# Splitting streamed weights into two parts: whole slots of 1024 columns instead of two halves

## The chip, the cores and the metric

The kernel runs on one core of one Trainium2 chip. The time is device microseconds of that core from the start to the end of one launch, the median of several executions. Before the change it is 2640.28 us (three runs, 2636.97 to 2641.47).

## What is computed

The reference is two transformer-like blocks in float32 over one sequence of 256 tokens and 1024 features, each of two layers. Cut to what matters here:

```
def first_block(x, mem, ...):
    for l in range(2):
        x = layer_norm(a * x + 0.5 * swiglu(x, ffn1_w1[l], ffn1_w3[l], ffn1_w2[l]))
        x = layer_norm(a * x + token_mixing(x, w_in[l], ...))       # gMLP, conv, MLA, NSA branches
        x = layer_norm(a * x + cross_attention(x, mem, ...))
        x = layer_norm(a * x + 0.5 * swiglu(x, ffn2_w1[l], ffn2_w3[l], ffn2_w2[l]))

def second_block(x, p, ...):
    for layer in range(2):
        x = half_ffn(x, ...)
        x = x + mixer(rmsnorm(x))          # layer 0: GLA + RG-LRU, layer 1: HGRN
        x = half_ffn(x, ...)
        x = x + sigmoid(rmsnorm(x) @ ple_gate[layer]) * (p[layer] @ ple_proj[layer])
    return rmsnorm(x)
```

Nearly all the work is products of the 256 x 1024 activations with weight matrices that are read once each from HBM: feed-forward matrices of 1024 x 2816 (24 of them), the input projection of token mixing, and smaller ones.

## The kernel before, in words

**Three products for one.** Products run in the type float32r. To keep float32 accuracy each operand is split into a part `hi` (the value cast to float32r) and a rest `lo` (value minus `hi`), and `mm3` (L187) computes hi·hi + hi·lo + lo·hi: L190, L191 and L192 are its three matmuls. Activations are split when they are transposed (`split_to`, L258; `rms_prep`, L327); weights are split as they stream in.

**Slots.** A slot is 128 partitions x up to 1024 columns of weights, 512 KB. `slot` (L167) starts the DMA on the SP queue into a raw buffer `raw` (pool of 4), ScalarE casts it into `whi` (L176) and VectorE subtracts into `wlo` (L177); both of these pools hold 8. Before the change each slot of n columns is split in two halves of n/2: cast, subtraction, cast, subtraction. A full slot feeds 12 matmuls of 512 columns: two k-blocks (or two column halves), two token tiles, three products.

**Token tiles.** The 256 tokens are two tiles t = 0, 1 of 128 rows. `lin` (L194) and `ffn` (L360) loop over slots and use each for both tiles. `lin_rows` (L224) makes the last product of a stage: it keeps the last `skew` slots, finishes tile 0, calls `done(0)`, and runs tile 1's share of these slots while tile 0 is normalised; then comes `done(1)`, while TensorE begins the next stage with tile 0's 24 matmuls.

**The end of a stage.** In the first block `done` is `layer_norm` (L293). On tile 1 it is a chain over four engines: two sums on VectorE (L299, one per half), the mean in two tiny steps (L302, L303), the sum of squares on ScalarE (`lnj`, L306), its scaling on VectorE (`rs`, L308), a power on GpSimd (L309), and the normalisation on VectorE, L313 with the mean and L314 with `rs`; then TensorE transposes (L318 here, L335 in `rms_prep`) and the result is split into `xT` (L259 and L260, or L339 and L340). In the second block `done` adds the residual, transposes, splits with a gain (`rms_prep`) and takes the sum of squares on ScalarE (`junk`, L325).

**Order.** The program is recorded in the order of the code and put in its final order, engine by engine, by a scheduler with its own estimates of durations; `issue_after` pins a few places. Each engine then works its list in order, so a weight cast or subtraction stands at a fixed place among the steps of a normalisation and everything behind it waits with it. Side work (attention, recurrences) is woven between slots by `weave` (L85).

Of the kernel before, what the change touches and what calls it, by code (L numbers as in the profile page):

```python
# [94 lines left out]
class Core:  # L95
    def __init__(self, tc, ctx, a):
        self.tc, self.a = tc, a
        nc = self.nc = tc.nc
        self.V, self.A, self.G, self.T = nc.vector, nc.scalar, nc.gpsimd, nc.tensor
        e = ctx.enter_context  # L100

        self.wsp = e(tc.tile_pool(name="wsp", bufs=8))
        self.xp = e(tc.tile_pool(name="xp", bufs=1))
        self.bp = e(tc.tile_pool(name="bp", bufs=11))
        self.cst = e(tc.tile_pool(name="cst", bufs=1))
        self.wraw = e(tc.tile_pool(name="wraw", bufs=4))
        self.rp = e(tc.tile_pool(name="rp", bufs=2))
        self.gbp = e(tc.tile_pool(name="gbp", bufs=1))
        self.sc2 = e(tc.tile_pool(name="sc2", bufs=6))
        self.sc4 = e(tc.tile_pool(name="sc4", bufs=2))  # L110
        self.biasp = e(tc.tile_pool(name="biasp", bufs=2))
        self.smp = e(tc.tile_pool(name="smp", bufs=5))
        self.accp = e(tc.tile_pool(name="accp", bufs=4, space=PSUM))
        self.atp = e(tc.tile_pool(name="atp", bufs=2, space=PSUM))
        self.tpp = e(tc.tile_pool(name="tpp", bufs=2, space=PSUM))
        self.ident = self.const("c_ident")
        self.mhalf = self.cst.tile([P, 32], F32, name="mhalf")
        self.V.memset(self.mhalf, -0.5)
        self.one = self.cst.tile([P, 1], F32, name="one")
        self.V.memset(self.one, 1.0)  # L120
# [46 lines left out]
    def slot(self, parts, n):  # L167

        raw = self.wraw.tile([P, 1024], F32, tag="raw", name="raw")
        hi = self.wsp.tile([P, 1024], F32R, tag="whi", name="whi")  # L170
        lo = self.wsp.tile([P, 1024], F32R, tag="wlo", name="wlo")
        for view, src in parts(raw):
            self.nc.sync.dma_start(out=view, in_=src)
        m = n // 2
        for v in (slice(0, m), slice(m, n)):
            self.A.copy(hi[:, v], raw[:, v])  # L176
            self.V.tensor_sub(lo[:, v], raw[:, v], hi[:, v].bitcast(F32))  # L177
        return hi, lo
# [1355 lines left out]
```

## Time and profile before

| | |
|---|---|
| median of three runs | 2640.28 us |
| the profiled execution | 2640.52 us |
| its span in the trace | 2638.7 us |
| TensorE busy in the span | 2597.5 us, 98% |
| VectorE busy | 1648.4 us, 62% |
| ScalarE busy | 1398.0 us, 53% |
| granted TensorE clock, mean | 0.997 |
| weight casts (L176) and subtractions (L177) | 1682 each |

The trace is of one execution. A group of instructions is named by its line in the code, its engine and the tiles it writes and reads; a duration of one instruction includes some latency that overlaps the next one, so a pair of two takes less than twice one. An engine's idle time is put down to what ended it. TensorE's matmuls overlap each other and their ends are modelled, so "busy" there says that the engine had work, not that it ran at its peak.

### The profile page before, as it was taken

What the parts mean: (1) busy time and instruction counts of PE and PEld (TensorE: products, weight loads), DVE (VectorE), ACT (ScalarE), POOL (GpSimd) and SP (SyncE); (2) the same over time, 40 slices, a digit from 0 to 9 for tenths busy, and PEclk for the clock granted to TensorE, in tenths of its full rate; (3) what the DMA queues carried; (4) which work ended last, traced back from release to release, by engine and by line L of the source; (5) the groups of instructions that cost most, each with busy time, mean ns of one, the idle gap of its engine ahead of it and who ended that gap; (6) DMA issues with size and microseconds to landing.
All of it is one profiled execution on the core that took longest, in us unless ns stands there. A gap on an engine that the chain in (4) does not pass through costs nothing.

```text
span 2638.7 us, 35816 instructions
## 1 busy us (share of the span) xinstructions
PE 2597.5 (98%) x12833; PEld 2141.8 (81%) x12833; DVE 1648.4 (62%) x3232; ACT 1398.0 (53%) x2795; POOL 76.2 (3%) x122
## 2 busy tenths in 40 slices
PE   8999999999999999999999999999999999999998
PEld 7888877887888889877878878887888788777887
DVE  6557676766556557677675565567655655565554
ACT  5445545555445445545565455456554655765544
POOL 0000000000000000001000000000000000001000
PEclk9999999999999999999999999999999999999999
DMA  8648564546657557554456556554655665455652
GB/s 282 186 157 225 169 187 128 155 152 196 188 168 215 184 168 218 163 169 132 135 182 195 191 174 193 195 168 130 181 185 172 199 184 197 146 166 146 188 191 96
DMA packets 261800, 465.42 MB, mean 176 GB/s; under 512 B 25963, under 2 KB 96118, under 8 KB 261622
## 3 DMA queue, kind: packets, MB, share of 16 engines
q1 hardware_dynamic: 261622, 463.13, 57.7%
q8 instruction: 101, 1.65, 0.3%
q14 instruction: 77, 0.63, 0.1%
HBM read 462.02 MB, written 1.05 MB: 175 GB/s over the span
## 4 chain that ended last, share of the span: by engine, by line
PE 88%; DVE 5%; ACT 3%; DMA 2%; issue 1%; POOL 1%; POOLq 0%; DVEq 0%; ACTq 0%; SPq 0%
PE h L190 11%; PE h L192 11%; PE h L191 11%; PE o L190 7%; PE o L191 7%; PE o L192 7%; PE lin L190 6%; PE lin L192 6%; PE lin L191 6%; PE tp L268 2%; PE linT L220 1%; PE linT L219 1%; PE linT L218 1%; PE sp L447 1%; DVE wlo L177 1%
## 5 line engine op out<-in xcount | busy, mean ns | idle before, releaser
L177 DVE TENSOR_TENSOR wlo<-raw,whi 128x512 fp32r<-128x512 f32 (+3 forms) x1682 | 1100.1, 688 | 723.2 <-ACT whi L176 719.7
L176 ACT CAST whi<-raw 128x512 fp32r<-128x512 f32 (+3 forms) x1682 | 963.6, 616 | 892.3 <-PE h L192 366.4
L190 PE MATMUL h<-whi,xT 128*128 128x512 f32 x1280 | 504.0, 394 | 2.4 <-ACT whi L176 1.2
L192 PE MATMUL h<-whi,xT 128*128 128x512 f32 x1280 | 499.5, 391 | 0.8 <-DVE xT L260 0.8
L191 PE MATMUL h<-wlo,xT 128*128 128x512 f32 x1280 | 499.1, 390 | 0.0
L190 PEld LDWEIGHTS h<-whi,xT 128*128 128x128 f32 x1280 | 240.8, 188 | 55.8 <-ACT xT L339 4.9
L192 PEld LDWEIGHTS h<-whi,xT 128*128 128x128 f32 x1280 | 240.6, 188 | 52.7 <-DVE xT L260 1.7
L191 PEld LDWEIGHTS h<-wlo,xT 128*128 128x128 f32 x1280 | 241.0, 188 | 48.6
L190 PE MATMUL o<-whi,gT 128*128 128x512 f32 x704 | 275.7, 392 | 0.0
L191 PE MATMUL o<-wlo,gT 128*128 128x512 f32 x704 | 275.4, 391 | 0.0
L192 PE MATMUL o<-whi,gT 128*128 128x512 f32 x704 | 274.8, 390 | 0.0
L190 PE MATMUL lin<-whi,xT 128*128 128x512 f32 (+2 forms) x656 | 263.0, 401 | 1.6 <-ACT xT L339 1.3
L192 PE MATMUL lin<-whi,xT 128*128 128x512 f32 (+2 forms) x656 | 258.3, 394 | 0.0
L191 PE MATMUL lin<-wlo,xT 128*128 128x512 f32 (+2 forms) x656 | 257.0, 392 | 0.0
L192 PEld LDWEIGHTS o<-whi,gT 128*128 128x128 f32 x704 | 132.2, 188 | 27.1
L190 PEld LDWEIGHTS o<-whi,gT 128*128 128x128 f32 x704 | 132.2, 188 | 26.8
L191 PEld LDWEIGHTS o<-wlo,gT 128*128 128x128 f32 x704 | 132.2, 188 | 26.4
L190 PEld LDWEIGHTS lin<-whi,xT 128*128 128x128 f32 x656 | 124.4, 190 | 27.6 <-ACT xT L339 2.5
L192 PEld LDWEIGHTS lin<-whi,xT 128*128 128x128 f32 x656 | 124.3, 190 | 24.4 <-issue 1.3
L191 PEld LDWEIGHTS lin<-wlo,xT 128*128 128x128 f32 x656 | 124.5, 190 | 22.4 <-issue 1.4
L218 PE MATMUL linT<-xT,whi 128*128 128x256 f32 (+1 forms) x264 | 75.0, 284 | 0.0
L220 PE MATMUL linT<-xT,wlo 128*128 128x256 f32 (+1 forms) x264 | 74.9, 284 | 0.0
(464 smaller groups left out, 3162.6 us busy)
## 6 DMA issues: line engine op xcount, KB each, us to landing
raw<-in_ffn_w SPq DMA_DIRECT2D x496, 512.0 KB
raw<-in_w_in SPq DMA_DIRECT2D x120, 512.0 KB
raw<-in_m_w_in SPq DMA_DIRECT2D x52, 512.0 KB
raw<-in_ffn_w SPq DMA_DIRECT2D x64, 256.0 KB
raw<-in_w_o SPq DMA_DIRECT2D x16, 512.0 KB
raw<-in_m_w_out SPq DMA_DIRECT2D x16, 512.0 KB
raw<-in_ple_gate SPq DMA_DIRECT2D x16, 512.0 KB
bias<-in_b_in SPq DMA_DIRECT2D x24, 256.0 KB
```

Of the source, the lines that this page charges most:

```text
L176: self.A.copy(hi[:, v], raw[:, v])
L177: self.V.tensor_sub(lo[:, v], raw[:, v], hi[:, v].bitcast(F32))
L190: mm(ps, xh, wh, start=start, stop=False)
L191: mm(ps, xh, wl, start=False, stop=False)
L192: return mm(ps, xl, wh, start=False, stop=stop)
L218: mm(ps[:m, :], wh[:, k, :], xh, start=(k == 0), stop=False)
L219: mm(ps[:m, :], wh[:, k, :], xl, start=False, stop=False)
L220: mm(ps[:m, :], wl[:, k, :], xh, start=False, stop=(k == nk - 1))
L268: self.T.transpose(tp[:, j, :], src[:, (b + j) * P:(b + j + 1) * P], self.ident)
L447: self.T.matmul(sp[:, j * w:(j + 1) * w], q_of(h), k_of(h)[:, 0:w], start=True, stop=True)
```

## The change

The second half of `slot` is rewritten: from the fifth slot on, one cast and one subtraction cover all n columns; the first four slots of the program keep two halves. DMAs, pools and matmuls are as before.

```diff
--- before.py
+++ after.py
@@ -113,6 +113,7 @@
         self.accp = e(tc.tile_pool(name="accp", bufs=4, space=PSUM))
         self.atp = e(tc.tile_pool(name="atp", bufs=2, space=PSUM))
         self.tpp = e(tc.tile_pool(name="tpp", bufs=2, space=PSUM))
+        self.nslot = 0
         self.ident = self.const("c_ident")
         self.mhalf = self.cst.tile([P, 32], F32, name="mhalf")
         self.V.memset(self.mhalf, -0.5)
@@ -171,8 +172,11 @@
         lo = self.wsp.tile([P, 1024], F32R, tag="wlo", name="wlo")
         for view, src in parts(raw):
             self.nc.sync.dma_start(out=view, in_=src)
-        m = n // 2
-        for v in (slice(0, m), slice(m, n)):
+
+        self.nslot += 1
+        m = n if self.nslot > 4 else n // 2
+        for c in range(0, n, m):
+            v = slice(c, c + m)
             self.A.copy(hi[:, v], raw[:, v])
             self.V.tensor_sub(lo[:, v], raw[:, v], hi[:, v].bitcast(F32))
         return hi, lo
```

The program now has 845 casts and 845 subtractions in place of 1682 each: 841 slots, 8 halves for the first four. Since the scheduler places every instruction by its estimates, the lists of all engines shift too. Three places matter below (line numbers behind the change are higher by 4).

VectorE at the entry of layer 0's token mixing, from tile 1's sums to its normalisation (`lny`, `mu`, `rs` and `x` are steps of the layer norm, `wlo` a weight subtraction); before:

```order
L177 TENSOR_TENSOR wlo<-raw,whi 128x512 x2
L299 SCALAR_TENSOR_TENSOR lny,sum<-x_136,o 128x512 x2
L177 TENSOR_TENSOR wlo<-raw,whi 128x512
L302 TENSOR_TENSOR mu<-sum 128x1
L177 TENSOR_TENSOR wlo<-raw,whi 128x512
L303 TENSOR_SCALAR mu<-mu 128x1
L177 TENSOR_TENSOR wlo<-raw,whi 128x512
L313 SCALAR_TENSOR_TENSOR x_1697<-lny,mu,G 128x512 x2
L308 TENSOR_SCALAR rs<-var 128x1
L177 TENSOR_TENSOR wlo<-raw,whi 128x512
L314 SCALAR_TENSOR_TENSOR x_1697<-x_1697,rs,B 128x512 x2
```

and now:

```order
L181 TENSOR_TENSOR wlo<-raw,whi 128x1024 x2
L303 SCALAR_TENSOR_TENSOR lny,sum<-x_136,o 128x512 x2
L181 TENSOR_TENSOR wlo<-raw,whi 128x1024
L306 TENSOR_TENSOR mu<-sum 128x1
L181 TENSOR_TENSOR wlo<-raw,whi 128x1024
L307 TENSOR_SCALAR mu<-mu 128x1
L317 SCALAR_TENSOR_TENSOR x_1573<-lny,mu,G 128x512 x2
L312 TENSOR_SCALAR rs<-var 128x1
L743 TENSOR_TENSOR zl<-lin,bias 128x416
L318 SCALAR_TENSOR_TENSOR x_1573<-x_1573,rs,B 128x512 x2
```

Before, three half subtractions stood between the sums (L299) and the first step of the normalisation (L313), two of them ahead of the mean (L303), and one 1024-column slot stood ahead of the sums. Now two whole slots stand ahead of the sums and two between the sums and the mean, so the mean comes behind the fourth 1024-column slot instead of the second.

ScalarE at the same place, from tile 0's sum of squares to tile 1's (`lnj`); before:

```order
L306 ACTIVATE lnj,var<-lny,mu 128x1024
L176 CAST whi<-raw 128x416 x4
L259 CAST xT<-tp 128x4x128 x2
L176 CAST whi<-raw 128x512 x7
L306 ACTIVATE lnj,var<-lny,mu 128x1024
```

and now:

```order
L310 ACTIVATE lnj,var<-lny,mu 128x1024
L180 CAST whi<-raw 128x832 x2
L263 CAST xT<-tp 128x4x128 x2
L180 CAST whi<-raw 128x1024 x4
L310 ACTIVATE lnj,var<-lny,mu 128x1024
```

Seven half casts of 512 columns stood before tile 1's `lnj`, three and a half slots; now it is four whole ones.

ScalarE at the entry of the second block's HGRN mixer, from the last casts before tile 1's transposed split `xT` on; before:

```order
L176 CAST whi<-raw 128x512 x2
L339 ACTIVATE xT<-tp,gcol 128x128
L176 CAST whi<-raw 128x512 x6
L339 ACTIVATE xT<-tp,gcol 128x128 x2
L325 ACTIVATE junk,ss<-x_20635 128x1024
L339 ACTIVATE xT<-tp,gcol 128x128 x2
```

and now:

```order
L180 CAST whi<-raw 128x1024
L343 ACTIVATE xT<-tp,gcol 128x128
L180 CAST whi<-raw 128x1024
L343 ACTIVATE xT<-tp,gcol 128x128
L180 CAST whi<-raw 128x1024 x2
L329 ACTIVATE junk,ss<-x_19193 128x1024
L343 ACTIVATE xT<-tp,gcol 128x128 x6
```

Before, the first two pieces of tile 1's `xT` came behind half of the sixth slot, and ahead of the sum of squares `junk`. Now they come behind the whole slot and behind `junk`.

## Rows read from the trace of the kernel before

**Rows 1.** The page, part 1: busy time (share of the span) and instructions of each engine.

```profile
PE 2597.5 (98%) x12833; PEld 2141.8 (81%) x12833; DVE 1648.4 (62%) x3232; ACT 1398.0 (53%) x2795; POOL 76.2 (3%) x122
```

**Rows 2.** The page, part 5: groups by line; busy us, mean ns of one | idle before.

```profile
L177 DVE TENSOR_TENSOR wlo<-raw,whi 128x512 fp32r<-128x512 f32 (+3 forms) x1682 | 1100.1, 688 | 723.2 <-ACT whi L176 719.7
...
L176 ACT CAST whi<-raw 128x512 fp32r<-128x512 f32 (+3 forms) x1682 | 963.6, 616 | 892.3 <-PE h L192 366.4
```

**Rows 3.** The view of waits, whole span: who waited for whom, us, times, longest.

```profile
ACT whi L176 <- PE h L192: 366.4, 258, 2.0
```

**Rows 4.** The same view for TensorE alone.

```profile
PE tp L318 <- DVE x L314: 10.1, 13, 1.9
...
PE h L190 <- ACT whi L176: 1.2, 1, 1.2
```

**Rows 5.** Timeline, entry of layer 0's token mixing: start, us, engine, line, [idle <-releaser].

```profile
202.44 0.62 ACT L176 CAST whi<-raw 128x512 fp32r<-128x512 f32 x1 [1.52 <-DMA raw<-in_w_in]
...
202.97 1.15 ACT L306 ACTIVATE lnj<-lny,mu 128x1024 f32<-128x1024 f32 x1
...
204.24 0.15 DVE L308 TENSOR_SCALAR rs<-var 128x1 f32<-128x1 f32 x1 [0.31 <-ACT lnj L306]
...
206.33 1.29 PE L318 MATMUL tp<-c_ident,x 128*128 128x128 f32 x8 [1.90 <-DVE x L314]
```

**Rows 6.** Timeline, entry of layer 1's token mixing.

```profile
979.68 0.62 ACT L176 CAST whi<-raw 128x512 fp32r<-128x512 f32 x1 [1.35 <-DMA raw<-in_w_in]
...
983.57 1.29 PE L318 MATMUL tp<-c_ident,x 128*128 128x128 f32 x8 [1.57 <-DVE x L314]
```

**Rows 7.** Groups by line and shape: operations of 1024 columns that are there already.

```profile
L1271 DVE TENSOR_TENSOR hlf<-hlf,lbd 128x1024 f32<-128x1024 f32 x2 | 2.4, 1220 | 0.0
...
L1270 ACT ACTIVATE hw<-hw 128x1024 f32<-128x1024 f32 x2 | 2.1, 1042 | 0.0
```

**Rows 8.** Timeline, entry of layer 0's second feed-forward.

```profile
790.38 0.62 ACT L176 CAST whi<-raw 128x512 fp32r<-128x512 f32 x1 [1.42 <-DMA raw<-in_ffn_w]
...
792.18 0.15 DVE L308 TENSOR_SCALAR rs<-var 128x1 f32<-128x1 f32 x1
```

**Rows 9.** Timeline, from the first block to the second.

```profile
1565.25 1.15 ACT L176 CAST whi<-raw 128x512 fp32r<-128x512 f32 x2 [0.91 <-DMA raw<-in_ffn_w]
...
1567.57 0.15 DVE L308 TENSOR_SCALAR rs<-var 128x1 f32<-128x1 f32 x1 [0.52 <-ACT lnj L306]
```

**Rows 10.** Timeline, entry of the second block's HGRN mixer.

```profile
2269.37 0.62 ACT L176 CAST whi<-raw 128x512 fp32r<-128x512 f32 x1 [1.89 <-DMA raw<-in_m_w_in]
...
2269.89 0.62 ACT L339 ACTIVATE xT<-tp,gcol 128x128 fp32r<-128x128 f32 x2
...
2270.40 1.06 ACT L325 ACTIVATE junk<-x 128x1024 f32<-128x1024 f32 x1
```

**Rows 11.** Timeline, from the embedding gate to the next feed-forward.

```profile
2073.96 1.29 DVE L177 TENSOR_TENSOR wlo<-raw,whi 128x512 fp32r<-128x512 f32 x2
...
2075.18 0.62 ACT L176 CAST whi<-raw 128x512 fp32r<-128x512 f32 x1 [0.73 <-DMA raw<-in_ffn_w]
...
2075.70 0.68 ACT L1448 ACTIVATE sgate<-o,rs 128x512 f32<-128x512 f32 x1
```

**Rows 12.** Timeline of TensorE alone, token mixing of layer 0.

```profile
332.13 0.39 PE L191 MATMUL lin<-wlo,xT 128*128 128x512 f32 x1
332.44 0.44 PE L462 MATMUL tp<-c_ident,smask 128*128 128x128 f32 x2
332.64 0.48 PE L192 MATMUL lin<-whi,xT 128*128 128x512 f32 x1
```

**Rows 13.** One stretch: its us; busy of PE, PEld, DVE, ACT, POOL; clock; DMA share; GB/s.

```profile
2280.00:2320.00 40.00, 40.00 (x178) 33.14 (x177) 25.88 (x38) 36.99 (x54) 0.00 (x0) 1.00 0.46 146
```

**Rows 14.** The view of waits, weight loads of TensorE: two steps of the attention branches.

```profile
PEld po L468 <- ACT pT L464: 7.9, 30, 0.7
...
PEld tp L462 <- ACT smask L458: 6.6, 20, 0.5
```

## The prediction

> **What bounds the kernel now.** Read the page's first part before anything else: TensorE has work for 2597.5 us of the 2638.7 us span, against 1648.4 us on VectorE and 1398.0 us on ScalarE [rows 1]. All its idle time together is 2638.7 - 2597.5 = 41.2 us. The change touches no matmul, so it can act only through this idle time and through the few places where TensorE's order shifts.
>
> Next, the groups by line. The two operations that the change merges are the largest users of their engines: 1682 subtractions, 1100.1 us, and 1682 casts, 963.6 us [rows 2]. Size is not weight on the path, so the view of waits comes third, and it reads in the other direction from what those sums suggest: 258 times, 366.4 us in total, a cast waited for TensorE to finish with an old weight buffer [rows 3]. The weights are ahead. TensorE waited for a cast just once, for 1.2 us [rows 4].
>
> What TensorE does wait for is the normalisation of tile 1 at the end of a stage: 13 waits, 10.1 us, the longest 1.9 [rows 4]. The timeline of the entry of layer 0's token mixing shows one of them whole. The weights of the fourth slot land, a cast that had waited 1.52 us for them starts at 202.44, the sum of squares `lnj` stands behind this cast in ScalarE's list and starts at 202.97, `rs` follows at 204.24, and TensorE resumes at 206.33 after 1.90 us of nothing [rows 5]. Layer 1 shows the same pattern with 1.35 us of waiting for the weights and 1.57 us of idle TensorE [rows 6]. A normalisation step here pays for a weight slot that it does not need, because the engine's list is in order.
>
> **The bulk of the change.** 837 slots change. Two half subtractions in a row take 1.29 us [rows 11], two half casts 1.15 us [rows 9]. For the whole ones no row has the same operation; the nearest are operations of 1024 columns on float32, 1.220 us on VectorE and 1.042 us on ScalarE [rows 7]. I take these. VectorE saves 837 x (1.29 - 1.22) = 59 us, ScalarE 837 x (1.15 - 1.04) = 92 us. Bounds: nothing saved at one end; at the other the 0.15 us that the shortest VectorE operation takes [rows 5] once per slot, 126 us. Either end is worth 0 us of time, since the casts wait for TensorE anyway [rows 3]. If that cover were gone, the slot's two operations in sequence would bind: 1.04 + 1.22 = 2.26 us before its first column can be used, in place of 0.62 + 0.69. A full slot feeds 12 matmuls, one per 0.227 us (two 512-column matmuls that follow each other directly in this kernel start that far apart; the row shown, 332.13 to 332.64, has two small transposes between), so TensorE draws on it for 2.7 us, and with buffers for eight slots the longer latency stays hidden in mid-stage. The raw buffer is freed some 0.35 us later (2.26 against 0.62 + 2 x 0.64 with the casts overlapped), which delays the DMA that SP has queued for it. That matters only where the casts already wait for a DMA; it goes into the upper end of the range. GpSimd's list has no weight work, and its order around the powers is unchanged.
>
> **The ends of stages.** Here one whole operation stands where one or two halves stood, and the sum is made of these.
>
> *Two mixing entries.* Now the mean stands behind the subtraction of the fourth whole slot. Its data land as before at 202.44 [rows 5]; the cast ends at 203.48, the subtraction near 204.7, the second step of the mean near 204.8. `lnj` starts at 204.84 in place of 202.97: +1.9 us. TensorE is already idle at this point, so all of it counts. Layer 1 has the same order [rows 6]. Together **+3.8**. The lower end is 0, if the slot lands 1.9 us sooner.
>
> *Second feed-forward of layer 0.* The cast at 790.38 is again one that waited for its DMA [rows 8]. Whole, it ends at 791.42, its subtraction at about 792.6, and one half of the normalisation's first step (L313) comes between that and `rs`: 793.2 in place of 792.18. **+1.0** (0 to 1.2).
>
> *First block to second.* The two half casts at 1565.25 become one that ends at the same time, so `lnj` stays where it was; but a whole subtraction of that slot now stands ahead of the first step of the normalisation. It ends near 1567.5, half of that step follows for 0.6, and `rs` starts near 1568.8 in place of 1567.57 [rows 9]. **+1.2** (0 to 1.4).
>
> *HGRN mixer.* Before, two pieces of `xT` were made at 2269.89, behind a half cast and ahead of `junk` [rows 10]. Now the whole cast ends at 2270.41 and `junk`, 1.04 us later, still goes first: `xT` starts at 2271.45, 1.56 later. **+1.5** (0.5 if TensorE has other matmuls for a microsecond, 1.8 with the rest of the pieces late).
>
> *Embedding gate to the next feed-forward.* The sigmoid waits for a whole cast in place of a half, 1.04 against 0.53 (2075.18 to 2075.70) [rows 11]: **+0.5**.
>
> *Four further second tiles* (the entry and the end of cross attention in both layers): no weight slot lands late there, and a step waits at most one half operation longer, 0 to 0.6 us each. I take 0.3: **+1.2**.
>
> Sum: 3.8 + 1.0 + 1.2 + 1.5 + 0.5 + 1.2 = **+9.2 us**.
>
> **What the change gives back.** In TensorE's list the switches between weight matmuls and others fall from 819 to 785, 17 excursions fewer. One excursion costs little: in the row shown, two matmuls with two small transposes between start 0.31 + 0.20 us apart in place of 0.227, and the transposes' own part of that, the 0.20 from 332.44 to 332.64, has to be paid anyway. That leaves 0.08 [rows 12], and 17 x 0.08 = **-1.4 us** (0 if the transposes fit between weight matmuls for nothing). Late in the HGRN mixer ScalarE is busy 36.99 of 40 us [rows 13], the one stretch where its work itself may hold something up; its 0.1 us per slot over the 14 slots of that stretch make 1.4 us, of which I take **-1.0** (0 to -1.4). The net is 9.2 - 1.4 - 1.0 = +6.8.
>
> The profiled execution took 2640.52 us, its span and 1.8 us around it, and stands 0.2 above the median of the runs, 2640.28. So 2640.5 + 6.8 = **2647.3 us**.
>
> **Rivals.**
>
> *No measurable change (a).* The delays at the later places are covered. For: at the second block's entries the new TensorE order puts six or seven weight matmuls ahead of tile 1's transposes where there were three, 0.7 to 0.9 us more to do while it waits. Against: at the mixing entries TensorE has run out of work for 1.90 and 1.57 us already [rows 5, 6]. Then only the 3.8 remain, and 2640.5 + 3.8 - 2.4 = 2641.9; with the mixing entries half covered also, 2640. Range 2640 to 2645.
>
> *Faster (b).* The relief reaches the chains that do hold TensorE. In the attention branches its weight loads wait 7.9 us for `pT` and 6.6 us for `smask`, both made on ScalarE [rows 14]. ScalarE has 92 us less to do and half as many weight operations in its list; if half of these 14.5 us goes and the ends of stages stay as they are, the time is 2640.5 - 7.3 - 1.4 = 2632. It decides if these steps mostly wait behind a second half cast of a pair; it fails if they wait behind the one that happens to run, since that one is now longer. The floor is set by the 41.2 us of all idle time.
>
> *Slower by more (c).* The same 50 waits grow instead [rows 14]: a step that becomes ready during a cast waits up to 1.04 - 0.62 = 0.42 us more, 50 x 0.42 = 21 us at most, 10.5 if half of them meet a cast. On top of my sum that is 2658. It speaks against it that ScalarE is only 53% busy [rows 1], so that the average step meets no cast at all. The Trainium skill, "Perfetto Trace Analysis", section "Optimizing Scalar/DVE Operations", takes this side: grouping into larger operations helps a saturated engine, but "If Scalar/Vector aren't saturated, but are causing bubbles on other engines, breaking up instructions may allow work to be completed sooner." By this rule the halves were right, and merging them lengthens every bubble; the trace agrees on its condition, with engines at 53% and 62%, and with bubbles that are few.
>
> That the change does not do what it says is excluded: the lists hold 845 casts and 845 subtractions.
>
> **How the numbers follow.** A measurement of this kernel can tell about 0.2%, 5.3 us, from no change. My sum, by itself good for 2645.6 to 2651, gets 0.41; (a) gets 0.36, as cover is easily overlooked at eight of the ten places; (b) 0.14; (c) 0.09. Faster by over 0.2% is (b), 0.14; within it (a), 0.36; slower the forecast and (c), 0.50. The range reaches down between (b) and (a), 2635, and up to just short of (c) at 2657, which takes in the upper ends of the places (0.2 + 0.2 + 0.3 + 1.2) and five raw buffers freed 0.35 late.
>
> **What would show it.** Right: 845 casts near 1.04 us and 845 subtractions near 1.22 us; matmuls still 12833; idle TensorE up from 41 to about 48 us, TensorE's idle time at the two mixing entries near 3.8 and 3.5 us, and `xT` at the HGRN entry late by 1.5. Wrong: waits there as before, or TensorE waiting for casts in mid-stage (the eight buffers would not cover), or a whole operation taking clearly more or less than the 1024-column rows; and a changed start-to-start time of matmuls, which nothing here accounts for.

## The result: 0.74% slower, and the profile after

The changed kernel takes 2659.06 us, median of four runs (2657.75 to 2663.33), against 2640.77 us: a ratio of 1.0074 (95% interval 1.0061 to 1.0087), 18.3 us slower. The forecast was 2647.3, the range ended at 2657. The direction was right, the size was not: the loss is 2.7 times the forecast one. One execution among all the runs below, the first profiled one of the kernel with whole casts and half subtractions, ran at a granted clock of 0.801 throughout and has no part in the ratios.

The page's first part and the two merged groups, behind the change:

```profile
PE 2601.9 (98%) x12833; PEld 2149.2 (81%) x12833; DVE 1591.3 (60%) x2395; ACT 1324.3 (50%) x1960; POOL 87.3 (3%) x122
...
L181 DVE TENSOR_TENSOR wlo<-raw,whi 128x1024 fp32r<-128x1024 f32 (+3 forms) x845 | 1024.8, 1216 | 770.4 <-ACT whi L180 767.1
...
L180 ACT CAST whi<-raw 128x1024 fp32r<-128x1024 f32 (+3 forms) x845 | 872.2, 1035 | 940.1 <-PE h L196 399.3
```

They answer to [rows 1, 2]. The profiled execution has a span of 2656.2 us, 17.5 longer. There are 845 casts of 1035 ns and 845 subtractions of 1216 ns, as the 1024-column rows had it [rows 7], and ScalarE and VectorE have 74 and 57 us less to do. None of that shortened anything. TensorE's idle time rose from 41.2 to 2656.2 - 2601.9 = 54.3 us, by 13.1, and its busy time by 4.4 with the same 12833 matmuls. That second part is the clock: the trace's record of the granted clock has 34.9 us at the half level (1.2 GHz), against 18.0 before, which by itself makes (34.9 - 18.0) / 2 = 8.4 us, if work at half the clock takes twice as long; some stretches elsewhere became shorter.

What ScalarE and TensorE wait for (the view of waits: us, times, longest):

```profile
ACT whi L180 <- PE h L196: 399.3, 263, 2.4
```

```profile
PE tp L322 <- DVE x L318: 15.3, 14, 3.3
...
PE po L472 <- ACT pT L468: 3.2, 4, 1.1
...
PE tp L694 <- ACT nqT L583: 3.1, 2, 2.1
...
PE hdec L1284 <- ACT hed L1286: 2.6, 1, 2.6
...
PE h L194 <- ACT whi L180: 1.2, 1, 1.2
```

The casts still wait for TensorE, 399 us [rows 3], and TensorE still waited once for a cast, 1.2 us [rows 4]: the eight buffers do cover the longer latency in mid-stage. The wait for the normalisation rose from 10.1 to 15.3 us [rows 4]. Three lines are new or much larger: `pT` and `nqT`, steps of the attention branches in token mixing, and `hed`, a step of the HGRN mixer.

The entry of layer 0's token mixing (timeline: start, us, engine, line, [idle before <- what ended it]):

```profile
200.82 1.05 ACT L180 CAST whi<-raw 128x1024 fp32r<-128x1024 f32 x1 [1.52 <-DMA raw<-in_w_in]
...
201.90 1.23 DVE L181 TENSOR_TENSOR wlo<-raw,whi 128x1024 fp32r<-128x1024 f32 x1 [0.70 <-ACT whi L180]
...
203.04 0.15 DVE L307 TENSOR_SCALAR mu<-mu 128x1 f32<-128x1 f32 x1
...
203.29 1.15 ACT L310 ACTIVATE lnj<-lny,mu 128x1024 f32<-128x1024 f32 x1 [1.42 <-DVE mu L307]
...
206.28 1.75 PE L322 MATMUL tp<-c_ident,x 128*128 128x128 f32 x8 [3.27 <-DVE x L318]
```

This is [rows 5] again, and step by step what was forecast: the cast waits 1.52 us for the DMA, the whole subtraction follows it, the mean stands behind that, and `lnj`, which began 0.53 us after the slot's cast began, now begins 2.47 us after it. TensorE is idle for 3.27 us instead of 1.90, so 1.4 of the 1.9 us reach it. (The whole place comes 1.4 us sooner in this trace: TensorE runs out of work at 203.01 instead of 204.43, and it resumes at 206.28, as it did before.) The other long entries are, in order of time, the place of [rows 8], layer 1's mixing [rows 6], and first block to second [rows 9]. (The place of [rows 8], at 790 us, is called the entry of layer 0's second feed-forward ahead and in the expectations; it is that stage's end, where layer 1 begins.) Two of them before, the third being in [rows 6]:

```profile
794.28 1.29 PE L318 MATMUL tp<-c_ident,x 128*128 128x128 f32 x8 [0.74 <-DVE x L314]
...
1569.57 1.32 PE L335 MATMUL tp<-c_ident,x 128*128 128x128 f32 x8 [1.20 <-DVE x L314]
```

and all three now:

```profile
799.87 1.72 PE L322 MATMUL tp<-c_ident,x 128*128 128x128 f32 x8 [2.06 <-DVE x L318]
...
992.18 1.09 PE L322 MATMUL tp<-c_ident,x 128*128 128x128 f32 x4 [3.23 <-DVE x L318]
...
1584.02 1.32 PE L339 MATMUL tp<-c_ident,x 128*128 128x128 f32 x8 [2.21 <-DVE x L318]
```

Idle time there was 0.74, 1.57 and 1.20 us; it is 2.06, 3.23 and 2.21. What had not been forecast follows directly behind these places. Stretches behind two of them (length; busy time of PE, PEld, DVE, ACT, POOL; granted clock; DMA share; GB/s):

```profile
206.60:210.10 3.50, 3.50 (x14) 2.90 (x13) 2.54 (x9) 1.18 (x2) 1.01 (x2) 0.51 0.86 299
...
800.50:804.00 3.50, 3.47 (x11) 2.92 (x12) 1.38 (x2) 1.17 (x2) 0.00 (x0) 0.51 0.92 307
```

The clock is at its half level for 3.4 us behind all four of these entries. TensorE is busy all that time at three of them; at layer 1's mixing the level falls before TensorE resumes, and 3.0 us of it are work. If this work would take half as long at full clock, that is another 1.7 us at three entries and 1.5 at the fourth, 6.6 us. Before, the clock fell three times in the whole program, at none of these places.

Nor had the attention branches of token mixing been in the sum. TensorE's idle stretches of 0.25 us and more in the two bodies were four before, 1.4 us together; now they are eight, 7.3 us. One place in layer 0, before:

```profile
409.99 0.69 DVE L177 TENSOR_TENSOR wlo<-raw,whi 128x512 fp32r<-128x512 f32 x1
...
410.59 0.16 DVE L455 TENSOR_SCALAR nb<-mx 128x4 f32<-128x4 f32 x1
...
413.80 0.27 PE L462 MATMUL tp<-c_ident,smask 128*128 128x128 f32 x1
...
414.37 0.40 PE L192 MATMUL lin<-whi,resa 128*128 128x512 f32 x1
414.75 1.10 PE L468 MATMUL po<-VV,pT 128*128 128x64 f32 x8
```

and now:

```profile
412.69 1.22 DVE L181 TENSOR_TENSOR wlo<-raw,whi 128x1024 fp32r<-128x1024 f32 x1
...
413.83 0.16 DVE L459 TENSOR_SCALAR nb<-mx 128x4 f32<-128x4 f32 x1
...
414.09 0.40 ACT L462 ACTIVATE smask<-smask,nb 128x128 f32<-128x128 f32 x1 [3.12 <-DVE nb L459]
...
414.63 1.48 PE L466 MATMUL tp<-c_ident,smask 128*128 128x128 f32 x4
...
415.64 1.03 ACT L180 CAST whi<-raw 128x1024 fp32r<-128x1024 f32 x1
...
416.57 0.57 ACT L468 COPY pT<-tp 128x512 f32<-128x512 f32 x1
...
417.20 1.10 PE L472 MATMUL po<-VV,pT 128*128 128x64 f32 x8 [1.09 <-ACT pT L468]
```

A softmax has two dependent steps on VectorE, the row maxima and their scaled negative `nb` (L455 before, L459 now). A half subtraction stood between them, now a whole one does, and a whole cast stands ahead of the copy to `pT`. Yet the chain is no longer than it was: from the start of the subtraction to the product with the values (`po`, L468 and L472) it took 4.76 us and takes 4.51, since the exponentials had waited for a half cast before. In all 36 such steps of token mixing together `nb` comes 17.8 us behind the maxima before and 18.3 now. What differs is TensorE's own list. Before, 21 weight matmuls stood between the scores and `po`, some of them between the four transposes of `smask` (L462) and three behind the last. Now the scheduler has put 12 there, all ahead of the transposes (L466), and TensorE has nothing left to do while `pT` is made: it is idle for 1.09 us, and the granted clock then falls to half for 6.8 us, from 418.3 on. Layer 1 has the same wait. For `nqT` it is ScalarE's list. Before, the last cast ahead of this copy was a half one that waited for no DMA; now it is a whole one that did:

```profile
360.79 1.05 ACT L180 CAST whi<-raw 128x1024 fp32r<-128x1024 f32 x1 [0.32 <-DMA raw<-in_w_in]
361.74 0.58 ACT L583 COPY nqT<-tp 128x512 f32<-128x512 f32 x1
```

How long the body of each token mixing takes can be read between two groups of transposes, those of tile 1 at its entry and those of tile 0 at its end. Layer 0 and layer 1, before:

```profile
541.41 0.63 PE L318 MATMUL tp<-c_ident,x 128*128 128x128 f32 x4 [0.56 <-DVE x L314]
...
1317.09 0.63 PE L318 MATMUL tp<-c_ident,x 128*128 128x128 f32 x4 [0.57 <-DVE x L314]
```

and now:

```profile
546.56 0.63 PE L322 MATMUL tp<-c_ident,x 128*128 128x128 f32 x4 [0.57 <-DVE x L318]
...
1330.14 0.63 PE L322 MATMUL tp<-c_ident,x 128*128 128x128 f32 x4 [0.57 <-DVE x L318]
```

With the starts in [rows 5, 6] and above, the bodies took 541.41 - 206.33 = 335.1 and 1317.09 - 983.57 = 333.5 us; they take 546.56 - 206.28 = 340.3 and 1330.14 - 992.18 = 338.0. That is +5.2 and +4.4 us (4.9 and 3.9 in an expectation below). Of these 9.6 us, 3.2 are the half level behind the two entries, counted above; the other 6.4, over a third of the whole loss, lie in a part of the program to which the prediction's sum gave nothing.

### The profile page after: what moved, and what is told of

Read it like the earlier page. It is cut to its first block, busy times and chain, and to the rows that moved or that the text cites. A ratio compares the mean times of both kernels' runs of the same rounds, so it can differ in the third digit from the quotient of the medians.

```text
span 2656.2 us, 34147 instructions
## 1 busy us (share of the span) xinstructions
PE 2601.9 (98%) x12833; PEld 2149.2 (81%) x12833; DVE 1591.3 (60%) x2395; ACT 1324.3 (50%) x1960; POOL 87.3 (3%) x122
## 4 chain that ended last, share of the span: by engine, by line
PE 88%; DVE 4%; ACT 3%; DMA 3%; issue 1%; POOL 1%; SPq 0%; DVEq 0%; POOLq 0%; ACTq 0%
PE h L194 11%; PE h L196 11%; PE h L195 11%; PE o L194 7%; PE o L195 7%; PE o L196 7%; PE lin L194 6%; PE lin L195 6%; PE lin L196 6%; PE tp L272 2%; PE linT L223 1%; PE linT L224 1%; PE linT L222 1%; PE sp L451 1%; DVE wlo L181 1%; ACT whi L180 1%
## 5 line engine op out<-in xcount | busy, mean ns | idle before, releaser
L181 DVE TENSOR_TENSOR wlo<-raw,whi 128x1024 fp32r<-128x1024 f32 (+3 forms) x845 | 1024.8, 1216 | 770.4 <-ACT whi L180 767.1
L180 ACT CAST whi<-raw 128x1024 fp32r<-128x1024 f32 (+3 forms) x845 | 872.2, 1035 | 940.1 <-PE h L196 399.3
L462 ACT ACTIVATE smask<-smask,nb 128x128 f32<-128x128 f32 (+1 forms) x96 | 42.7, 446 | 68.1 <-DVE nb L459 68.1
```

The lines of the kernel that those rows point to most:

```text
L462: self.A.activation(sm[:, j * w:(j + 1) * w], sm[:, j * w:(j + 1) * w], AF.Exp, bias=nb[:, j:j + 1], scale=scale, accum_out=den[:, j:j + 1])
```

## The experiments

Ratios are against runs of the kernel before on the same chip, with 95% intervals. In diffs, `fresh` counts the slots of a stage, down from 8 in the first ones and up from 0 in the deferral; lines that repeat are shown once. Each edit also makes the scheduler place everything anew, so lists shift that the edit doesn't name. Each trace is of one execution, which can lie anywhere in the spread of its kernel.

**Halves back in places.** First at the start of every stage, then in all of token mixing, then both.

```diff
-        m = n if self.nslot > 4 else n // 2
+        self.fresh -= 1
+        m = n if self.nslot > 4 and self.fresh < 0 else n // 2
...
+            k.fresh = 8
             memT = k.mixing(l, xT, done)
```

> The changed kernel, but the first eight slots of each of the 16 stages (124 slots, 15% of all) are split in halves again. Theory: whole operations stand in the chain of tile 1's normalisation, at the stage entries, and the longer idle time there is followed by a stretch at half clock. The stage entries gave +1.7, +2.2 (mixing), +1.6 and +1.1 (second feed-forward of layer 0), +1.0 and +1.5 (first block to second), and two half-clock stretches of 1.7 us each behind the mixing entries: 12.5 us come back, 2659 - 12.5 = 2646.5 (2644 to 2650), and the idle time at the mixing entries is 1.9 and 1.6 us again instead of 3.3 and 3.2. Rival (the loss is spread over the program, by the scheduler's new order or by the longer wait for each slot): at most 15% of 18.5 us comes back, 2656 to 2659.

Measured: 2649.57 us, 1.0034 (1.0021 to 1.0047). Half of the loss is gone with 15% of the slots, and the idle time at the mixing entries is 2.17 and 1.50 us, with no half level behind any of the four long entries. The spread loss of the rival is excluded; the loss sits at places.

```diff
-        m = n if self.nslot > 4 else n // 2
+        m = n if self.nslot > 4 and not self.inmix else n // 2
...
+            k.inmix = True
             memT = k.mixing(l, xT, done)
+            k.inmix = False
```

> The changed kernel, but all slots of the two token mixings are split in halves again (200 slots, 24%). Theory: besides the entries (1.7 + 2.2), the side chains of the attention branches wait behind whole operations, which made the two bodies 4.9 and 3.9 us longer, half-clock stretches among it: 12.6 us come back, 2646.5 (2644 to 2650), and TensorE's waits of 1.1 us for pT and 2.1 us behind nqT are gone. Rival (loss in proportion to the slots): 24% of 18.5 us, 2654.6.

Measured: 2643.92 us, 1.0016 (1.0008 to 1.0025). Token mixing with its entries carries most of the loss, a little more than expected, and the waits for `pT` and `nqT` are below 0.3 us. The entries did not come back as a whole: TensorE's idle time there is 2.58 and 1.50 us in this trace, and the half level still follows the first.

Both edits together:

```diff
-        m = n if self.nslot > 4 else n // 2
+        self.fresh -= 1
+        m = n if self.nslot > 4 and self.fresh < 0 and not self.inmix else n // 2
```

> The changed kernel with halves both in the first eight slots of every stage and in all of token mixing; 527 slots of the feed-forwards and of the second block's mixers stay whole. Theory (whole operations cost only at the ends of stages and in the attention branches): 2642 (2639 to 2645), the kernel before up to the wait for the HGRN mixer's decay (hdec), which is 2.6 us in the changed kernel against 0.4. Rival (every whole slot costs a little): 527 of 837 slots keep 11.6 us of 18.5, 2651.

Measured: 2644.11 us, 1.0020 (1.0010 to 1.0029). 527 whole slots in the feed-forwards and the second block cost about 5 us together (2.6 to 7.7 by the interval), and the rival of 11.6 is out. That this is no better than halves in token mixing alone was not expected. The profiled executions differ by 6 us (spans 2638.4 and 2644.3), but one is among the fastest of its kernel and the other among the slowest; the medians do not differ. It stays open.

**Is it the place in the list?** Nothing is cut smaller here; the splits of a new stage's slots 5 to 8 are only queued behind tile 1's sum of squares (`sq`, ScalarE) and its scaling (`rv`, VectorE).

```diff
+        if t == 1:
+            self.fresh, self.held = 0, (sq, rv)
...
+        self.fresh += 1
+        with ExitStack() as held:
+            if 5 <= self.fresh <= 8:
+                held.enter_context(self.tc.issue_after(self.held[0].ins))
+                held.enter_context(self.tc.issue_after(self.held[1].ins))
...
```

> The changed kernel, all slots whole as they are, but at the end of each stage of the first block the splits of the new stage's slots 5 to 8 are queued behind tile 1's sum of squares (on ScalarE) and its scaling (on VectorE). Theory (the place in the in-order list costs, not the size of the operation): the stage entries lose their delays though nothing is cut smaller. The excess idle at four entries (6.4 us) and the four half-clock stretches behind them (6.8) go, and some of the idle time that the kernel before has there too (1.9, 1.6): 2643 (2640 to 2648), idle TensorE at the mixing entries under 1.5 us. Rival (the whole operation's latency costs, or TensorE needs these slots early): no gain, 2657 to 2663, with waits for whi behind the entries.

Measured: 2647.29 us, 1.0031 (1.0019 to 1.0043), at the slow end of the expectation. The whole operations are as long as before, and the normalisation no longer pays for them: the idle time at the mixing entries is 0.65 and 0.66 us, less than in either kernel. What was not foreseen is where a part of it went. In the changed kernel with the deferral TensorE waits for another step of VectorE a little later in token mixing:

```profile
PE lin L200 <- DVE R L751: 3.9, 2, 2.9
```

one of them 2.9 us long, behind layer 1's entry, and the clock falls behind it too.

The same edit in the kernel before, around its two halves:

> The kernel before (halves everywhere) with the same deferral of slots 5 to 8. Theory: the idle time at the ends of the first block's stages (1.9, 1.6, 1.2, 0.9, 0.8, 0.7 us) shrinks by about half, 4 to 5 us: 2636 (2633 to 2639). Rival: these waits are of the chain's own length and not of the splits in it, 2640 to 2642; or weights come late, over 2643.

Measured: 2632.86 us, 0.9980 (0.9971 to 0.9988). The kernel before paid at these places as well, with its halves. In its trace with the deferral the entry of layer 0's mixing reads:

```profile
200.26 1.16 ACT L313 ACTIVATE lnj<-lny,mu 128x1024 f32<-128x1024 f32 x1 [4.92 <-DVE mu L310]
...
203.25 0.63 PE L327 MATMUL tp<-c_ident,x 128*128 128x128 f32 x4 [0.65 <-DVE x L323]
```

`lnj` waits for the mean alone, the cast comes behind it, and TensorE's 1.90 us of idle time are 0.65. **This version is faster than both kernels.**

**Which of the two operations?**

```diff
-            self.V.tensor_sub(lo[:, v], raw[:, v], hi[:, v].bitcast(F32))
+            for d in range(c, c + m, n // 2):
+                u = slice(d, d + n // 2)
+                self.V.tensor_sub(lo[:, u], raw[:, u], hi[:, u].bitcast(F32))
```

> Whole casts, but each subtraction in two halves again. Theory (both engines' lists carry steps of the same chains): about half the loss stays, 2650 (2646 to 2655); at the mixing entries the mean stands behind one half subtraction less, so the idle time there is about 2.6 us instead of 3.3. Rival (one engine does it all): if VectorE, 2640 to 2642; if ScalarE, 2657 to 2660.

And the mirror image:

```diff
-            self.A.copy(hi[:, v], raw[:, v])
+            for d in range(c, c + m, n // 2):
+                u = slice(d, d + n // 2)
+                self.A.copy(hi[:, u], raw[:, u])
```

> Half casts, but one whole subtraction per slot. Theory: the other half of the loss, 2649 (2645 to 2654), with the waits for pT and nqT (both copies of ScalarE) as in the kernel before, and the idle time at the mixing entries near 2.6 us. Rival (one engine does it all): if ScalarE, 2640 to 2642; if VectorE, 2657 to 2660.

Measured: whole casts alone 2640.74 us, 1.0009 (0.9999 to 1.0019); whole subtractions alone 2661.72 us, 1.0098 (1.0083 to 1.0113). My theory, half each, is wrong, and the rival that named VectorE is right: whole subtractions by themselves cost as much as the change does (the two intervals overlap). For a trace of whole casts the kernel was run a second time.

> Whole casts and half subtractions once more, for a trace at full clock. Theory as it now stands (the loss is VectorE's whole subtraction alone, since the steps that a normalisation or a softmax takes between two subtractions can then only go after a whole one): 2641 (2638 to 2644); idle time at the mixing entries 1.9 and 1.6 us as in the kernel before, no waits of 1 us for pT. Rival (the whole cast costs as well, and something else gave it back): the waits of the changed kernel at these places, and an idle time in total well above 41 us with a gain elsewhere.

Measured: 2642.06 us, 1.0017 (1.0008 to 1.0026). The entry of layer 0's mixing with whole casts and half subtractions:

```profile
201.65 0.69 DVE L183 TENSOR_TENSOR wlo<-raw,whi 128x512 fp32r<-128x512 f32 x1
...
202.20 1.05 ACT L180 CAST whi<-raw 128x1024 fp32r<-128x1024 f32 x1 [1.14 <-DMA raw<-in_w_in]
...
202.25 0.15 DVE L309 TENSOR_SCALAR mu<-mu 128x1 f32<-128x1 f32 x1
...
203.15 1.15 ACT L312 ACTIVATE lnj<-lny,mu 128x1024 f32<-128x1024 f32 x1
...
206.52 1.29 PE L324 MATMUL tp<-c_ident,x 128*128 128x128 f32 x8 [1.69 <-DVE x L320]
```

and the same place with half casts and whole subtractions:

```profile
202.25 1.22 DVE L183 TENSOR_TENSOR wlo<-raw,whi 128x1024 fp32r<-128x1024 f32 x1 [0.21 <-ACT whi L182]
...
203.40 0.15 DVE L309 TENSOR_SCALAR mu<-mu 128x1 f32<-128x1 f32 x1
...
206.63 1.46 PE L324 MATMUL tp<-c_ident,x 128*128 128x128 f32 x8 [2.79 <-DVE x L320]
```

With half subtractions the mean is finished at 202.40, behind two of them; the whole cast lets `lnj` begin 0.95 us after its own start instead of 0.53, and TensorE is idle for 1.69 us, no more than before. With whole ones the mean waits for the subtraction of a slot that has just landed, and the idle time is 2.79 us. The whole cast is not free everywhere: in the HGRN mixer the wait for `hed` is 3.8 us in this trace, and the clock is at its half level in 17 of the 24 us from there on, so the 0.1 to 0.2% that whole casts cost may be there. Other traces bear out the wait: it is 2.5 to 3.8 us in all eleven with whole casts in this mixer, and 0.1 to 0.4 in those with halves of both (2.2 with the deferral in the second block). The time at half level in this stretch varies from 3.4 to 17.1 us among the eleven, and no run changed the casts there alone.

**Finer still.** Whole casts, subtractions in quarters (`n // 4` in the edit above).

> Whole casts, subtractions in four quarters. Theory (the granularity of VectorE's list is what counts, and a finer one helps further): idle time at the stage ends shorter by 0.3 us each at some 15 places, 2637 (2634 to 2640). Rival (halves are fine enough: the mean already stands behind one half): 2640 to 2643, the subtractions' busy time up by some 200 us without effect.

Measured: 2642.76 us, 1.0017 (1.0009 to 1.0026), the same as with halves. By the time the rival is right. At the mixing entries the theory came true: TensorE's idle time there is 0.43 and 0.46 us, against 1.69 and 1.61 with halves. But its idle time in total is 46.9 us against 46.5, and at the entries of cross attention 1.84 and 2.28 us stand now instead of 0.98 and 1.49; what the finer pieces gain at one place is lost at others.

**How does VectorE's subtraction do it at the stage ends?** Two steps that depend on each other leave a gap between them, and in VectorE's lists a subtraction stands in it (the change's order rows show it between L306 and L307). This edit makes the mean of a layer norm in one step instead of two and so takes one gap away.

```diff
-        self.V.tensor_add(mu[:, 0:1], sm[:, 0:1], sm[:, 1:2])
-        self.V.tensor_scalar_mul(mu[:, 1:2], mu[:, 0:1], -1.0 / D)
+        self.V.tensor_scalar(mu[:, 1:2], sm[:, 0:1], sm[:, 1:2], -1.0 / D, op0=ALU.add, op1=ALU.mult)
```

> The changed kernel with the mean of a layer norm in one VectorE step instead of two dependent ones, so that no subtraction can be put between them. Theory (what a whole subtraction costs is paid once per gap between two dependent VectorE steps of a chain, as it is what the scheduler fills that gap with): at the four long entries lnj starts 1.4 us sooner and the normalisation ends about 0.8 us sooner, 3 us, and where that shortens the idle time below 2.5 us some of the half clock behind it goes: 2653 (2650 to 2656). Rival (a subtraction costs wherever it stands in the list, the gaps have no part): 2658 to 2660, since the number of subtractions ahead of the normalisation is the same.

Measured: 2653.74 us, 1.0058 (1.0045 to 1.0071). At the mixing entry:

```profile
201.31 0.20 DVE L306 TENSOR_SCALAR mu<-sum 128x1 f32<-128x1 f32 x1
...
201.50 1.23 DVE L181 TENSOR_TENSOR wlo<-raw,whi 128x1024 fp32r<-128x1024 f32 x1
...
201.61 1.16 ACT L309 ACTIVATE lnj<-lny,mu 128x1024 f32<-128x1024 f32 x1
...
205.46 1.29 PE L321 MATMUL tp<-c_ident,x 128*128 128x128 f32 x8 [1.96 <-DVE x L317]
```

The same subtractions are in the list, but the second one stands behind the mean, and `lnj` runs beside it. TensorE is idle for 1.96 us instead of 3.27; at the other three long entries it is 1.55, 2.54 and 0.99 instead of 2.06, 3.23 and 2.21. That is 3.7 us less idle time, and the median is 5.3 us lower, 4.2 by the ratios; the intervals of the two ratios overlap, so the trace carries this verdict and not the time alone. Two tiny operations became one, and what they gain is what no longer fits between them.

The same edit in the kernel before, and in the kernel before with the deferral:

> The kernel before with the mean in one step. Theory: the same gap, filled with half a slot, was worth 0.6 us at most where the sum of squares then starts sooner, and nothing where it stands behind a cast that waits for its DMA, as at the mixing entries: 2638 (2636 to 2640). Rival: no difference, 2640.

> The kernel before, with slots 5 to 8 of the first block's stages deferred and the mean in one step. With the subtractions already out of the chain the gap is empty, and the step saves its own latency, about 0.1 us at eight places: 2632.5 (2630 to 2635), the deferral's own time.

Measured: 2636.82 us, 0.9987 (0.9978 to 0.9995), and 2632.80 us, 0.9979 (0.9970 to 0.9988). With the subtractions out of the chain the gap is worth nothing, as expected. With half subtractions in it, it is worth 0.13%, a little more than expected and, within the intervals, as much as with whole ones (1.0074 to 1.0058); that a gap costs in proportion to what fills it is not shown by the times.

**And in the attention branches?** All casts whole, subtractions in halves in token mixing alone.

```diff
-            self.V.tensor_sub(lo[:, v], raw[:, v], hi[:, v].bitcast(F32))
+            q = n // 2 if self.inmix else m
+            for d in range(c, c + m, q):
+                u = slice(d, d + q)
+                self.V.tensor_sub(lo[:, u], raw[:, u], hi[:, u].bitcast(F32))
```

> The changed kernel, all casts whole, with subtractions in halves in the two token mixings alone (200 slots). Theory (VectorE's whole subtraction is the cost, in the attention branches as at the entries): as with both in halves there, 2644 (2641 to 2647). Rival (in the attention branches it is the whole cast in front of pT and nqT that holds TensorE, and VectorE costs only at the stage entries): the bodies stay 8.8 us longer, 2652 to 2656.

Measured: 2644.73 us, 1.0019 (1.0011 to 1.0028), as with both in halves there. `pT` and `nqT` are no longer among the waits of TensorE of 0.3 us or more, though whole casts still stand in front of both. The bodies are 332.5 and 336.0 us long (from the same two groups of transposes), against 340.3 and 338.0, although the clock is at half level for 6.8 us of the second. So in the attention branches too the loss needs whole subtractions and not whole casts. How they bring it about is another matter than at the stage ends: in the softmax shown above, TensorE's list has 21 weight matmuls between the scores and `po` again, six behind the last transpose (15 and none with whole subtractions alone). What came back with the half subtractions is the order that the scheduler gives to TensorE; no run held that order fixed and changed the subtraction's size alone.

**The clock, and what did not help.** Eight more transposes in each tile-1 normalisation of the first block, on values that nobody uses.

```diff
+        if t == 1:
+            for h in range(2):
+                tp = self.tp()
+                for j in range(4):
+                    self.T.transpose(tp[:, j, :], junk[:, (4 * h + j) * P:(4 * h + j + 1) * P], self.ident)
```

> The changed kernel with eight more transposes on TensorE in each tile-1 normalisation of the first block; they read the sum-of-squares scratch, whose values nobody uses, so they run in the idle time while TensorE waits. Theory (idle time of 2 us and more at a stage entry is followed by half clock, which costs another 1.7 us): the stretches at half clock behind the two mixing entries, the second feed-forward of layer 0 and the second block's entry are gone, 4 x 1.7 = 6.8 us less; where TensorE hardly waits the eight cost up to 0.3 us, about 1.2 us in all: 2653.5 (2651 to 2656). Rival (the clock falls there for another reason): the stretches stay and the time is 2659 to 2662.

Measured: 2658.27 us, 1.0081 (1.0067 to 1.0095). Half right. At the four entries the clock no longer falls; the stretch behind layer 0's mixing entry, to be held against 206.60 to 210.10 above:

```profile
208.00:212.00 4.00, 3.52 (x19) 2.60 (x18) 2.67 (x9) 1.50 (x3) 1.08 (x2) 1.00 0.76 271
```

The idle time of 3.27 us had become two of 1.35 and 0.61 with transposes between. But 64 transposes were added, four of the eight groups fall where TensorE was idle for less than 0.8 us, and the clock fell at three other places (397, 1206 and 2097 us) where it hadn't in the changed kernel. In the trace TensorE's idle time is 4.5 us less and its busy time 7.8 us more, where a cost of 1.2 had been expected. The time did not move.

The expectation's theory of the clock does not hold as a rule either. At such entries in the other traces, idle times of 2.17 us (halves at the ends), 2.27 us (half subtractions in token mixing) and 2.96 us (whole subtractions alone) were not followed by the half level, while 1.59 and 1.67 us (half subtractions in token mixing) and 1.81 us (the kernel before with the mean in one step) were. So 1.7 us behind each long entry is what the changed kernel's one trace shows, and not a fixed price.

The deferral in the second block also, in the kernel before:

```diff
-                self.A.mul(hi, tp[:, j, :], gcol[:, k:k + 1])
-                self.V.scalar_tensor_tensor(lo, tp[:, j, :], gcol[:, k:k + 1], hi.bitcast(F32),
-                                            op0=ALU.mult, op1=ALU.subtract)
+                sa = self.A.mul(hi, tp[:, j, :], gcol[:, k:k + 1])
+                sv = self.V.scalar_tensor_tensor(lo, tp[:, j, :], gcol[:, k:k + 1], hi.bitcast(F32),
+                                                 op0=ALU.mult, op1=ALU.subtract)
+        if t == 1:
+            self.fresh, self.held = 0, (sa, sv)
```

> The kernel before with slots 5 to 8 of a stage deferred, in the second block also (there behind the last piece of tile 1's xT). Theory: the entries of the second block's stages lose about half of their 1.4, 0.9 and 0.4 us as well: 2632 (2629 to 2635). Rival (weights come late there, as TensorE needs slots 5 to 8 before it has worked off what it holds): 2635 to 2642 with waits for whi.

Measured: 2634.52 us, 0.9989 (0.9979 to 0.9998). No better than the deferral in the first block alone; the second block's share gives nothing that can be told.

And the deferral of the first block with whole casts and half subtractions:

> Whole casts, half subtractions, and the deferral of slots 5 to 8 in the first block. Theory (the cast's size is indifferent): as the kernel before with the deferral, 2633 (2630 to 2637). Rival (a whole cast that is deferred comes late): 2638 or more.

Measured: 2637.10 us, 0.9997 (0.9988 to 1.0006), just beyond the expected 2630 to 2637 and between theory and rival; whole casts give back what the deferral gains, to 0.2%.

## Why the prediction was right and wrong

*That the bulk is worth nothing* was right: 74 and 57 us of engine time were saved, and TensorE's one wait for a cast is the same 1.2 us, with no new ones in mid-stage. (The view of waits before names a cast once more, 0.7 us ahead of `gdec` in the second block, which reads no weights.)

*The ends of stages.* The mechanism was right, and the terms were near: idle time at the two mixing entries +1.4 and +1.7, 3.0 us where 3.8 were forecast (`lnj` was 1.9 us late in layer 0, as forecast, but not all of it became idle time); the place of [rows 8] +1.3 (1.0 forecast); first block to second +1.0 (1.2); gate +0.4 (0.5); the four further tiles +0.5 (1.2). The HGRN entry was mis-sized: idle time of 0.96 us instead of 1.26, where +1.5 was forecast.

```profile
2284.76 1.05 ACT L180 CAST whi<-raw 128x1024 fp32r<-128x1024 f32 x1 [1.64 <-DMA raw<-in_m_w_in]
...
2286.76 0.61 ACT L343 ACTIVATE xT<-tp,gcol 128x128 fp32r<-128x128 f32 x2
```

`xT` begins 2.00 us after the cast that waited for its DMA instead of 0.52 [rows 10], 1.5 later, as forecast. But this cast begins 2.1 us after the stage's first matmul instead of 3.1, and TensorE has eleven weight matmuls before its wait instead of six, 0.8 us more work: the cover that rival (a) had named. Together the ends are 6.0 us instead of 9.2.

*The step that failed* is the sum's account of what else can hold TensorE. It priced the shift in TensorE's order only as a gain, -1.4 for 17 excursions fewer, and it gave the attention branches nothing. They cost 6.4 us, and where that could be followed it came from the lists: the transposes of a softmax in one block with no weight matmul behind it, and a cast that waits for its DMA ahead of `nqT`. The prediction had put the branches into rival (c), with a chance of 0.09 because ScalarE is only 53% busy. The time that (c) gave, 2658, is nearly the one measured, 2659.06, but that is luck: its mechanism was not at work. It let the 50 waits of [rows 14] grow by 10.5 us; they are 40 now, and 12.8 us instead of 14.5.

```profile
PEld po L472 <- ACT pT L468: 6.9, 18, 1.3
...
PEld tp L466 <- ACT smask L462: 5.9, 22, 0.4
```

What came instead are few waits, up to 2.1 us long, at new places, and a whole cast costs 0.1 to 0.2% in all. A busy share says nothing of either mechanism, since neither comes about by chance: the scheduler decides what stands between two dependent steps and what TensorE has left to do meanwhile. The sentence of the Trainium skill, "Perfetto Trace Analysis", section "Optimizing Scalar/DVE Operations", that breaking up may help where engines cause bubbles without being saturated, held for VectorE (1.0098 whole) and hardly for ScalarE (1.0009 to 1.0017).

*The clock* had no term at all. Idle time was priced at its own length; in the changed kernel's trace the half level behind the four long entries took a further 6.6 us, and over the program it took 8.4 us more than before.

*The HGRN mixer* was to gain 1.0 us by ScalarE's relief [rows 13]. Its wait for `hed` grew from 0.4 to 2.6 us instead. With whole subtractions alone it is 1.3, with whole casts alone 3.8: which points to the length of the casts in ScalarE's list and not to their sum; it was not tested alone.

Added up: 6.0 at the ends, 6.4 in the attention branches (half level among it), 6.6 of half level behind the four long entries and 2.2 in the HGRN mixer make 21.2; 3.7 us of gains, spread over the start, cross attention and other stretches, leave the 17.5 of the two spans.

## What to carry to other kernels

Merging operations that are off the critical path saves nothing there, and each merged one is a longer block that may end up between two steps of a chain: look at what an in-order list puts into the gaps of dependent steps, engine by engine, before asking how busy the engine is. Where a chain ends a stage, keeping unrelated work behind it (0.2% here) or taking a step out of the chain (0.13%) gained time, and cutting the unrelated work finer than a half did not. Where a scheduler places everything by its estimates, compare the list of the bottleneck engine too: the work that covered a wait may have moved. And price an idle stretch of TensorE together with the granted clock behind it, knowing that one trace shows it for one execution only.

## What had not been expected of the hardware

The granted clock explains most of the spread between runs of one and the same kernel. The 104 runs of the kernel before that were made beside the experiments, by the mean granted clock of the run:

| granted clock | runs | mean us |
|---|---|---|
| 0.998 | 52 | 2637.2 |
| 0.997 | 33 | 2639.5 |
| 0.996 | 12 | 2642.0 |
| 0.995 | 3 | 2644.3 |

(The other four, at 0.999, have a mean of 2637.1.) A thousandth of clock is worth 2.4 us, about a thousandth of the time, as is to be expected where TensorE is busy 98%. The changed kernel's runs stood at 0.992 to 0.994. And two operations of nearly equal length, 1.04 us on ScalarE and 1.22 on VectorE, that look alike in every total, differ widely in what their merging costs: 0.1 to 0.2% and 1.0%.
